# The up projection of a gated feed-forward block by Strassen's seven products of quarters

## The chip, the cores and the metric

The kernel runs on one core of one Trainium2 chip. Its engines are TensorE (PE; weight loads are shown as PEld), VectorE (DVE), ScalarE (ACT), GpSimd (POOL) and SyncE (SP, which here only issues DMAs). The metric is the device time of one execution in microseconds (us), lower is better. A matmul takes a stationary operand of 128x128 (the weights), a moving operand of 128 rows by some columns, and adds into PSUM.

## The reference, cut to what matters

One decoder layer is run for 512 prompt tokens and 64 sample tokens (8 sequences of 8), 576 columns in all. The model width is 1024 and D_FF is 2816. After retention, attention and the output projection comes the block that the change is about:

```
h = _rmsnorm(x, norm2_w)
ua, ub = jnp.split(h @ w_up, [D_FF], axis=-1)
buf = jnp.concatenate([conv_s0.astype(ua.dtype), ua], axis=1)
conv = conv_b
for j in range(CONV_W):
    conv = conv + buf[:, j:j + T] * conv_w[j]
x = x + (jax.nn.silu(conv) * ub) @ w_down
```

The outputs also hold the last two rows of `buf` (the convolution state) and a final norm of x.

## The kernel before, in words

All activations are kept transposed: 128 features on the partitions, 576 tokens along the free axis. A product in float32 is made of three passes of fp32r matmuls: both operands are split into a high part, rounded to fp32r, and the rest; high by high, high by low and low by high are added in PSUM.

Weights come as chunks of 128 columns by up to eight k tiles of 128 rows (`wraw`, 512 KB, three buffers). ACT rounds a chunk to `whi` (`w_split_hi`, L219) and DVE subtracts it from the raw one to make `wlo` (`w_split_lo`, L229), one chunk ahead of its use. `dense` (matmuls at L254) runs over the k tiles of a chunk: three passes by two halves of 288 tokens, six matmuls for each k.

The feed-forward block is done in two halves of 11 row tiles of D_FF each. For each tile f, called a slab here, `up` makes two dense products of eight k tiles, ua and ub: 2 x 48 = 96 matmuls. `up_post` then works on them beside the next slab: DVE scales ua by the norm's factor into `ue` (L1122, L1123), ACT and DVE do the three taps of the convolution (`cv`: L1126, L1130, L1131), ACT the silu (L1133); DVE scales ub into `g` (L1138), POOL multiplies it by the silu (L1141, L1142; DVE in the last slab of a half), ACT rounds the product (L1144) and DVE takes the rest (L1146). POOL also copies the convolution state in and out of `ue` (L1121, L1127, L1128). After 11 slabs, eight dense products with `w_down` (11 k tiles each) are added to x. The last of them, `last_down` (L1213), is cut into two groups of tokens so that the final norm overlaps it. `conv_state_in` (L1055) and `conv_state_out` (L1160) transpose the convolution state on PE.

The order of the work is fixed when the program is built: every engine has one queue and runs it in order, and semaphores hold an instruction back until what it reads is there and what it overwrites is no longer needed. The class `Merge` makes this order. It walks over generators that emit instructions and yield estimates of the time that PE and the other engines need, and lets the stream go on that is ready by these estimates. The run decides only the waits, not the order.

Of the kernel before, what the change touches and what calls it, by code (L numbers as in the profile page):

```python
# [18 lines left out]
P = 128  # L19
D = 1024  # L20
# [126 lines left out]
def decoder_step(ctx, tc, a):  # L147
# [29 lines left out]
    # ---- weights, streamed in order of use  # L177
# [3 lines left out]
    chunks = []  # L181
    IN_ORDER = [4 * sec + hp for hp in range(4) for sec in (1, 2, 0)]
    IN_ORDER += [4 * sec + hp for hp in range(4) for sec in (5, 4, 6)]
    IN_ORDER += [12 + hp for hp in range(4)]
    for m in IN_ORDER:
        chunks.append((("in", m, 0), a["w_in"], m, 0, 8))
    for m in range(8):
        chunks.append((("out", m, 0), a["w_out"], m, 0, 8))
    NFH = 11
    for half in range(2):  # L190
        for f in range(half * NFH, (half + 1) * NFH):
            chunks.append((("up", f, 0), a["w_up"], f, 0, 8))
            chunks.append((("up", NF + f, 0), a["w_up"], NF + f, 0, 8))
        for m in range(8):
            k0 = half * NFH
            chunks.append((("down", m, k0), a["w_down"], m, k0, k0 + 6))
            chunks.append((("down", m, k0 + 6), a["w_down"], m, k0 + 6, k0 + 11))
    raw, split = {}, {}
    state = {"load": 0, "use": 0}

    def w_load(upto):
        while state["load"] < min(upto, len(chunks)):
            w_load_part(state["load"], 0, 8)
            state["load"] += 1

    def w_load_part(i, c0, c1):
        _, w, m, k0, k1 = chunks[i]
        if i not in raw:
            raw[i] = wp.tile([P, 8, P], F32, name="wraw", tag="wraw", bufs=3)
        c1 = min(c1, k1 - k0)  # L210
        sp.dma_start(raw[i][:, c0:c1], wsrc(w, m, k0 + c0, k0 + c1))

    def w_split_hi(i, c0=0, c1=None):
        if i >= len(chunks) or i in split and c0 == 0:
            return
        if i not in split:
            split[i] = [wp.tile([P, 8, P], F32R, name="whi", tag="whi", bufs=2), None]
        c = slice(c0, c1 or chunks[i][4] - chunks[i][3])
        act.activation(split[i][0][:, c], raw[i][:, c], AF.Copy)  # L219

    def w_split_lo(i, c0=0, c1=None):
        if i >= len(chunks) or split[i][1] is not None and c0 == 0:
            return
        if split[i][1] is None:
            split[i][1] = wp.tile([P, 8, P], F32R, name="wlo", tag="wlo", bufs=2)
        hi, lo = split[i]
        n = chunks[i][4] - chunks[i][3]
        c = slice(c0, c1 or n)
        dve.tensor_sub(lo[:, c], raw[i][:, c], f32(hi[:, c]))  # L229
        if c.stop == n:  # L230
            raw.pop(i)

    def w_split(n):
        for i in range(state["use"], n):
            w_split_hi(i)
            w_split_lo(i)

    def w_next(key):
        i = state["use"]
        assert chunks[i][0] == key, (chunks[i][0], key)  # L240
        w_split(i + 1)
        state["use"] += 1
        return i, split.pop(i)

    def dense(ps, key, xhi, xlo, k0, k1, first, last, rows=None, made=None):
        """ps[:, C0 + n] (+)= sum over k of w[k, cols]^T x[k, n], in three exact-split passes."""
        i, (hi, lo) = w_next(key)
        w_split_hi(i + 1)
        for k in range(k0, k1):
            while made is not None and k not in made:  # L250
                yield None
            for wt, x in ((hi, xhi), (hi, xlo), (lo, xhi)):
                for s in range(2):
                    pe.matmul(ps[:, C0 + s * H2:C0 + (s + 1) * H2], wt[:, rows[k] if rows else k - k0], x[k][:, s * H2:(s + 1) * H2],  # L254
                              start=first and k == k0 and wt is hi and x is xhi,
                              stop=last and k == k1 - 1 and wt is lo)
            if k == k0 + 1:
                w_split_lo(i + 1)
            if k == k0 + 3:
                w_load(i + 4)  # L260
            yield 738.0, 0.0
# [4 lines left out]
    # ---- constants  # L266
# [31 lines left out]
    def rsqrt_steps(dst, v, t):  # L298
        """dst = v ** -0.5 for positive v: a seed from the exponent, then Newton's steps; t: scratch."""
# [24 lines left out]
    # ================= first norm  # L324
# [104 lines left out]
    def w_first():  # L429
        for i, h in ((0, 0), (1, 0), (0, 1), (1, 1)):  # L430
            w_split_hi(i, 4 * h, 4 * h + 4)
            yield 0.0, 700.0
            w_split_lo(i, 4 * h, 4 * h + 4)
            wk.add((i, h))
            yield 0.0, 900.0
# [3 lines left out]
    def in_first():  # L439
        """the first two tiles of columns advance together as x arrives"""  # L440
# [4 lines left out]
        for _, _, i, k in steps:  # L445
            while k not in split_k or (i, k // 4) not in wk:
                yield None
            hi, lo = split[i]
            for wt, x in ((hi, xhis), (hi, xlos), (lo, xhis)):
                for s in range(2):  # L450
                    pe.matmul(ps[i][:, C0 + s * H2:C0 + (s + 1) * H2], wt[:, k], x[k][:, s * H2:(s + 1) * H2],  # L451
                              start=k == 0 and wt is hi and x is xhis, stop=k == KD - 1 and wt is lo)
            if k == KD - 1:
                state["use"] += 1
                split.pop(i)
                if i == 0:
                    w_split_hi(2)
                    w_split_lo(2)
# [7 lines left out]
        yield from dense(first[m], ("in", m, 0), xhis, xlos, 0, KD, True, True)  # L466
# [8 lines left out]
    # ================= input projection, retention and dilated attention, by pairs of heads  # L475
# [13 lines left out]
    def natural(src, dst):  # L489
        """dst [token, tile, 128] = the transpose of src [128 features, T]"""  # L490
# [82 lines left out]
    def in_proj():  # L573
        for m in IN_ORDER:
# [3 lines left out]
            else:  # L578
# [3 lines left out]
                for c in dense(ps, ("in", m, 0), xhis, xlos, 0, KD, True, True):  # L582
# [9 lines left out]
    # ---- retention  # L592
# [12 lines left out]
    def retention():  # L605
        for hp in range(4):
# [13 lines left out]
            # scores, transposed: [key, query]  # L620
# [19 lines left out]
            # states after each chunk  # L640
# [13 lines left out]
            # outputs  # L654
# [21 lines left out]
            # group norm; the decay of a row only scales its statistics  # L676
# [29 lines left out]
            # states of the sample group  # L706
# [11 lines left out]
            # gate  # L718
# [13 lines left out]
    # ---- dilated attention, prompt  # L732
# [85 lines left out]
    def k_split(hp):  # L818
        """[k hi; k lo] of each head"""
# [26 lines left out]
    # ---- dilated attention, sample: four sequences at a time, each in 32 columns of the tensor engine  # L846
# [476 lines left out]
```

## Time and profile before

| what | us |
|---|---|
| three runs | 836.5, 838.94, 840.68; median 838.94 |
| span of the profiled execution | 838.0 |
| output projection | from about 345 to 396 |
| up, first half | from 396 to about 541 |
| down, first half | about 541 to 612 |
| up, second half | about 612 to 753 |
| down, second half | about 753 to 826 |
| final norm and last store | to 838.0 |

The page gives the profiled execution no time other than its span, which lies 0.9 us below the median of the runs. The slices of the page show PE busy at nine tenths or more nearly everywhere, and its granted clock at full except for one slice. Busy PE time counts the latency of overlapped matmuls too, so the pace is read from the count of matmuls in a stretch and not from the duration of one. An idle engine costs nothing unless another one waits for it.

### The profile page before, as it was taken

The numbers are of one execution on the slowest core, as the hardware profiler recorded it, in microseconds if no ns is written. First come the engines' busy times: TensorE is split into PE (matmuls) and PEld (weight loads), VectorE is DVE, ScalarE is ACT, GpSimd is POOL, SyncE is SP. The second block draws the span as 40 slices with busy tenths as digits, with TensorE's granted clock in tenths as the row PEclk, the third lists the DMA queues.
The fourth block names the chain that finished last, engine by engine and source line by source line (L and its number), as shares of the span: only waits on it lengthen the run. The fifth ranks groups of instructions, "written<-read, shape, count | busy, mean of one in ns | idle before, by whom it ended". The sixth has DMA issues, their size and how long they took to land.

```text
span 838.0 us, 16048 instructions
## 1 busy us (share of the span) xinstructions
PE 817.6 (98%) x6594; PEld 775.0 (92%) x6594; DVE 414.1 (49%) x796; ACT 295.2 (35%) x511; POOL 148.4 (18%) x234
## 2 busy tenths in 40 slices
PE   7999999998999999999999999999999999999995
PEld 6999999886887888999999999999999999999995
DVE  5664655655556456544555455432235545545333
ACT  5322321544536367234223333311223323332222
POOL 1312111020111113022212222100012222210111
PEclk9999999999999999899999999999999999999999
DMA  9355562667796873555256544453334445553213
GB/s 268 104 167 163 162 201 70 184 187 217 201 251 184 237 201 85 109 176 169 84 179 198 176 158 138 135 170 87 94 101 156 146 152 176 170 169 81 70 51 114
DMA packets 179534, 128.68 MB, mean 154 GB/s; under 512 B 15425, under 2 KB 176101, under 8 KB 178914
## 3 DMA queue, kind: packets, MB, share of 16 engines
q1 hardware_dynamic: 178308, 93.75, 40.1%
q10 hardware_dynamic: 928, 33.63, 11.0%
q8 instruction: 52, 0.85, 0.4%
q0 software_dynamic: 224, 0.28, 0.1%
q14 instruction: 22, 0.18, 0.1%
HBM read 121.52 MB, written 39.66 MB: 192 GB/s over the span
## 4 chain that ended last, share of the span: by engine, by line
PE 92%; DMA 3%; DVE 1%; ACT 1%; SPq 1%; issue 1%; POOL 0%; ACTq 0%; DVEq 0%; POOLq 0%
PE d L254 72%; PE m L877 2%; PE d L451 2%; PE m L923 2%; DMA kc<-in_cache_win_k_dram 1%; PE m L791 1%; PE d L887 1%; PE m L495 1%; PE m L804 1%; PE px L410 1%; PE m L1213 1%; PE px L254 1%; DMA csn<-in_state_conv_dram 1%; PE m L663 1%; PE m L764 1%
## 5 line engine op out<-in xcount | busy, mean ns | idle before, releaser
L219 ACT ACTIVATE whi<-wraw 128x1024 fp32r<-128x1024 f32 (+2 forms) x114 | 110.8, 972 | 372.2 <-issue 182.1
L229 DVE TENSOR_TENSOR wlo<-wraw,whi 128x1024 fp32r<-128x1024 f32 (+2 forms) x114 | 126.8, 1112 | 119.8 <-ACT whi L219 116.8
L254 PE MATMUL d<-bhi,whi 128*128 128x288 f32 x768 | 174.6, 309 | 0.0
L254 PE MATMUL d<-bhi,wlo 128*128 128x288 f32 x768 | 165.0, 297 | 0.0
L254 PE MATMUL d<-blo,whi 128*128 128x288 f32 x768 | 164.8, 296 | 0.0
L254 PE MATMUL d<-hhi,whi 128*128 128x288 f32 x704 | 150.9, 296 | 0.0
L254 PE MATMUL d<-hlo,whi 128*128 128x288 f32 x704 | 150.8, 296 | 0.0
L254 PE MATMUL d<-hhi,wlo 128*128 128x288 f32 x704 | 150.7, 296 | 0.0
L254 PEld LDWEIGHTS d<-bhi,whi 128*128 128x128 f32 x768 | 122.4, 191 | 5.3 <-issue 3.6
L254 PEld LDWEIGHTS d<-bhi,wlo 128*128 128x128 f32 x768 | 124.1, 189 | 0.0
L254 PEld LDWEIGHTS d<-blo,whi 128*128 128x128 f32 x768 | 124.1, 190 | 0.0
L254 PEld LDWEIGHTS d<-hhi,whi 128*128 128x128 f32 x704 | 113.4, 189 | 0.1
L254 PEld LDWEIGHTS d<-hhi,wlo 128*128 128x128 f32 x704 | 113.4, 189 | 0.0
L254 PEld LDWEIGHTS d<-hlo,whi 128*128 128x128 f32 x704 | 113.4, 189 | 0.0
L1122 DVE TENSOR_TENSOR ue<-d,rstd_b 128x512 f32<-128x512 f32 x22 | 15.2, 691 | 74.5 <-PE d L254 74.5
L1141 POOL TENSOR_TENSOR g<-g,cv 128x512 f32<-128x512 f32 x20 | 25.8, 1290 | 142.5 <-DVE g L1138 137.1
L785 POOL TENSOR_SCALAR s<-s,sc 128x128 f32<-128x128 f32 (+3 forms) x32 | 18.2, 578 | 141.7 <-DVE sc L783 140.4
L1038 POOL TENSOR_TENSOR acc<-acc,sq 128x576 f32<-128x576 f32 x13 | 21.4, 1646 | 111.5 <-ACT sq L1037 111.5
L1127 POOL COPY cout<-ue 128x2 f32<-128x2 f32 x22 | 5.7, 259 | 137.6 <-DVE ue L1122 137.6
L877 PE MATMUL m<-ident,kc 128*128 128x128 f32 x192 | 27.5, 277 | 2.1 <-DMA kc<-in_cache_win_k_dram 2.1
L878 DVE COPY kt<-m 128x384 f32<-128x384 f32 x32 | 17.8, 556 | 23.2 <-PE m L877 22.6
L878 ACT COPY kt<-m 128x384 f32<-128x384 f32 x32 | 15.3, 477 | 38.5 <-PE m L877 38.0
(261 smaller groups left out, 1033.7 us busy)
## 6 DMA issues: line engine op xcount, KB each, us to landing
wraw<-in_w_up_dram SPq DMA_DIRECT2D x44, 512.0 KB
wraw<-in_w_in_dram SPq DMA_DIRECT2D x26, 512.0 KB
kc<-in_cache_win_k_dram SPq DMA_DIRECT2D x32, 256.0 KB
vc<-in_cache_win_v_dram SPq DMA_DIRECT2D x32, 256.0 KB
wraw<-in_w_down_dram SPq DMA_DIRECT2D x16, 384.0 KB
wraw<-in_w_down_dram SPq DMA_DIRECT2D x16, 320.0 KB
kc<-in_cache_win_k_dram SPq DMA_DIRECT2D x64, 64.0 KB
vc<-in_cache_win_v_dram SPq DMA_DIRECT2D x64, 64.0 KB
```

What stands on the lines that cost most here:

```text
L219: act.activation(split[i][0][:, c], raw[i][:, c], AF.Copy)
L229: dve.tensor_sub(lo[:, c], raw[i][:, c], f32(hi[:, c]))
L254: pe.matmul(ps[:, C0 + s * H2:C0 + (s + 1) * H2], wt[:, rows[k] if rows else k - k0], x[k][:, s * H2:(s + 1) * H2], start=first and k == k ...
L410: pe.transpose(ps[:, s], xn[:r, j, k * P:(k + 1) * P], ident[:r, :r])
L451: pe.matmul(ps[i][:, C0 + s * H2:C0 + (s + 1) * H2], wt[:, k], x[k][:, s * H2:(s + 1) * H2], start=k == 0 and wt is hi and x is xhis, stop ...
L785: pool.tensor_scalar(s[:, :n], s[:, :n], c[:, 2:3], 1.0, op0=OP.mult, op1=OP.mult)
L877: pe.transpose(ps[:, j * P:(j + 1) * P], K[u, x][:, 3 * w + j], ident)
L878: (act.copy if w else dve.tensor_copy)(kt[:, w * 384:w * 384 + 384], ps[:, :384])
L923: pe.matmul(ps[x * 32:(x + 1) * 32, :P], pt[:n, j, x * 32:(x + 1) * 32], v, start=j == 0, stop=j == 6, tile_position=(0, x * 32))
L1038: pool.tensor_tensor(acc, acc, sq, op=OP.add)
L1122: dve.tensor_mul(u[:, 2:NP + 2], ya[:, :NP], rstd_b[:, :NP])
L1141: eng.tensor_tensor(g[:, :NP], g[:, :NP], c[:, :NP], op=OP.mult)
```

## The change: what it does

The up projection of a slab is taken as a 2x2 product of matrices. The weights are cut into A11 and A12 (k tiles 0 to 3 and 4 to 7 for ua) and A21 and A22 (the same for ub); h is cut into B11 and B12 (k tiles 0 to 3, token halves) and B21 and B22 (k tiles 4 to 7). Seven products of quarters (Winograd's form of Strassen's scheme), each of four k tiles by three passes by 288 tokens, take the place of eight. This needs four sums of weight quarters for each slab (S1 to S4, on POOL, `w_sum`) and four sums of quarters of h (T1 to T4, made once in `out_post`, on POOL, for the last pair of tiles on DVE). Results are put together from PSUM by three copies on ACT (`ct`) and three additions on DVE (into `y` and `z`; `z` is shown as `g`), partly while PE goes on adding to the same tile of PSUM.

Weights are split in quarters of four k tiles (128x512) throughout, two ahead and three in the feed-forward block, with five tiles for `whi` and `wlo` and a fourth raw buffer there. The down projection is done after 6, 14 and 22 slabs in chunks of 6, 8 and 8 k tiles, not twice 11. The output projection takes its tiles in the order 0, 4, 1, 5, 2, 6, 3, 7. The two copies of the convolution state into `cout` move from POOL to ACT, and its transposes become 4 on the way in and 5 on the way out in place of 22 and 22. `nfw`, the final norm's weight, is loaded before the last down stage and no longer before the output projection.

```diff
+    OUT_ORDER = [0, 4, 1, 5, 2, 6, 3, 7]
+    CHUNKS = [(0, 6), (6, 14), (14, 22)]
...
+    def add_slab(f):
...
+        quarters.extend([(i, slice(0, 4)), (i, slice(4, 8)), ("S2", f), ("S1", f), ("S3", f), ("S4", f),
+                         (i + 1, slice(4, 8))])
+        reads[i], reads[i + 1] = 5, 3
+        for n, which in enumerate(("S1", "S2", "S3", "S4")):
+            sums.setdefault(j - 5 + n, []).append((which, f, i))
...
+    def w_sum(which, f, i):
+
+        A11, A12, A21, A22 = raw[i][:, 0:4], raw[i][:, 4:8], raw[i + 1][:, 0:4], raw[i + 1][:, 4:8]
+        if which == "S3":
+            S[which, f] = A21
+            pool.tensor_tensor(A21, A11, A21, op=OP.subtract)
+            w_read(i)
             return
...
+        s = S[which, f] = state["ffn"][0].tile([P, 4, P], F32, name="ws", tag="ws", bufs=4)
+        if which == "S1":
+            pool.tensor_tensor(s, A21, A22, op=OP.add)
+            w_read(i + 1)
+        elif which == "S2":
+            pool.tensor_tensor(s, S["S1", f], A11, op=OP.subtract)
+            w_read(i)
+        else:
+            pool.tensor_tensor(s, A12, S["S2", f], op=OP.subtract)
+            w_read(i)
...
+    def w_begin(j):
+        for which in sums.pop(j, []):
+            w_sum(*which)
+        while state["hi"] <= min(j + ahead_of(), len(quarters) - 1):
+            if state["lo"] < state["hi"]:
+                w_lo(state["lo"])
+                state["lo"] += 1
+            w_hi(state["hi"])
+            state["hi"] += 1
...
+    def up(f, n, ghi, glo, made):
+
+        j = keys["up", f]
+        d, e = dtile(), mtile()
+        pa, pb, pc = d[:, :H2], d[:, 512:512 + H2], e[:, :H2]
+        y, z = tmp("y"), tmp("g")
+        ts = [fp.tile([P, H2], F32, name="ct", tag="ct", bufs=4) for _ in range(3)]
+        stage = []
+        for q, (dst, c) in enumerate(zip((pa, pb, pa, pc, pa, pc, pa), BQ)):
+            w_begin(j + q)
...
+                for wt, b in ((hi, xh), (hi, xl), (lo, xh)):
+                    pe.matmul(dst, wt[:, k], b[:, k], start=q in (0, 1, 3) and k == 0 and wt is hi and b is xh,
+                              stop=k == 3 and wt is lo, skip_group_check=True)
+                if k == 0:
+                    w_mid(j + q)
+                yield 385.0, 0.0
+            if q == 0:
+                act.copy(ts[0], pa)
+            elif q == 1:
+                dve.tensor_tensor(y[:, :H2], pb, ts[0], op=OP.add)
+            elif q == 2:
+                act.copy(ts[1], pa)
+            elif q == 3:
+                act.copy(ts[2], pc)
+            elif q == 4:
+                dve.tensor_tensor(z[:, H2:T], pa, ts[2], op=OP.add)
+            elif q == 5:
+                dve.tensor_tensor(y[:, H2:T], pc, ts[1], op=OP.add)
+                mg.add(up_post(f, n, pa, y, z, stage, ghi, glo, made), None, 4000.0 if f == 0 else 0.0)
+        stage.append(1)
...
-        dve.tensor_mul(u[:, 2:NP + 2], ya[:, :NP], rstd_b[:, :NP])
-        dve.tensor_mul(seqs(u, 2, TS), by_seq(ya[:, NP:]), by_seq(rstd_b[:, NP:]))
-        yield 0.0, 1800.0
-        c = fp.tile([P, UE], F32, name="cv", tag="cv", bufs=2)
+        dve.tensor_mul(u[:, 2:NP + 2], y[:, :NP], rstd_b[:, :NP])
+        dve.tensor_mul(seqs(u, 2, TS), by_seq(y[:, NP:T]), by_seq(rstd_b[:, NP:]))
+        yield 0.0, 1100.0
+        c = tmp("cv")
         act.activation(c[:, :L], u[:, 0:L], AF.Identity, scale=convw[:, 0, f:f + 1], bias=convb[:, f:f + 1])
-        pool.tensor_copy(cout[:, f, 0:2], u[:, NP:NP + 2])
-        pool.tensor_copy(by_seq(cout[:, f, 2:]), seqs(u, TS, 2))
-        yield 0.0, 1800.0
+        act.copy(cout[:, 0:2, f], u[:, NP:NP + 2])
+        act.copy(by_seq(cout[:, 2:, f]), seqs(u, TS, 2))
+        while not stage:
+            yield None
+        dve.tensor_mul(z[:, :H2], pa, rstd_b[:, :H2])
+        dve.tensor_mul(z[:, H2:T], z[:, H2:T], rstd_b[:, H2:])
+        yield 0.0, 900.0
```

VectorE's queue over one slab of the first up stage before (`wlo` is the low part of a weight chunk, `ue` the scaled ua, `cv` the convolution, `g` the scaled ub, `blo` the low part of the product):

```order
L1122 TENSOR_TENSOR ue1_4418<-d_5340,rstd_b_73 128x512
L1123 TENSOR_TENSOR ue1_4418<-d_5340,rstd_b_73 128x8x8
L229 TENSOR_TENSOR wlo_5418<-wraw_5307,whi_5401 128x1024
L1146 TENSOR_TENSOR blo_4932<-g_5364,bhi_4930 128x576
L1130 SCALAR_TENSOR_TENSOR cv_5435<-ue1_4418,vec_71,cv_5435 128x592
L1131 SCALAR_TENSOR_TENSOR cv_5435<-ue1_4418,vec_71,cv_5435 128x592
L229 TENSOR_TENSOR wlo_5483<-wraw_5372,whi_5468 128x1024
L1138 TENSOR_TENSOR g_5491<-d_5400,rstd_b_73 128x576
```

And now, from one slab's last convolution step to the next one's scaling of `y` (`ws` is a sum of weight quarters, `d` and `m` are PSUM, `y` and `ct` are in SBUF):

```order
L1271 SCALAR_TENSOR_TENSOR cv_5790<-ue1_4543,vec_71,cv_5790 128x592
L290 TENSOR_TENSOR wlo_5827<-wraw_5565,whi_5822 128x512
L1241 TENSOR_TENSOR y_5796<-d_5794,ct_5798 128x288
L290 TENSOR_TENSOR wlo_5847<-ws_5750,whi_5842 128x512
L290 TENSOR_TENSOR wlo_5868<-wraw_5565,whi_5863 128x512
L290 TENSOR_TENSOR wlob_5888<-wraw_5606,whib_5883 128x512
L1281 TENSOR_TENSOR blo_5141<-g_5644,bhi_5140 128x576
L1247 TENSOR_TENSOR g_5797<-d_5794,ct_5800 128x288
L290 TENSOR_TENSOR wlo_5909<-wraw_5606,whi_5904 128x512
L1249 TENSOR_TENSOR y_5796<-m_5795,ct_5799 128x288
L290 TENSOR_TENSOR wlo_5928<-ws_5861,whi_5923 128x512
L1258 TENSOR_TENSOR ue0_4541<-y_5796,rstd_b_73 128x512
```

Eight instructions of a slab have become seventeen: behind these rows follow the rest of `ue`, one more `wlo`, the two scalings of `g` and the two convolution steps (L1270, L1271). The scaling of `ue` reads SBUF twice now, where before one operand was in PSUM. On ACT the order there is `cv` (L1262), two copies into `cout`, the next `whi`, the first `ct`, another `whi`, the silu (L1273), another `whi`, the second `ct` (L1243).

GpSimd's queue over one slab before (`cout` is the convolution state out):

```order
L1141 TENSOR_TENSOR g_5491<-g_5491,cv_5435 128x512
L1142 TENSOR_TENSOR g_5491<-g_5491,cv_5435 128x64
L1121 COPY ue0_4416<-csT_4413 128x8x2
L1127 COPY cout_4414<-ue0_4416 128x2
L1128 COPY cout_4414<-ue0_4416 128x16
```

And now, in the slab whose rows of VectorE stand above:

```order
L269 TENSOR_TENSOR ws_5840<-wraw_5717 128x512
L1276 TENSOR_TENSOR g_5644<-g_5644,cv_5790 128x512
L1277 TENSOR_TENSOR g_5644<-g_5644,cv_5790 128x64
L272 TENSOR_TENSOR ws_5861<-ws_5840,wraw_5606 128x512
L264 TENSOR_TENSOR wraw_5717<-wraw_5606,wraw_5717 128x512
L275 TENSOR_TENSOR ws_5902<-wraw_5606,ws_5861 128x512
L1257 COPY ue0_4541<-csT_4525 128x8x2
```

The product for slab f now stands between the first sum of a slab and the other three, and the copy into `ue`, which `cv` on ACT waits for, stands behind the last sum.

## Rows read from the trace of the kernel before

**Rows 1.** The page's parts 1 and 4: busy time of each engine; the chain by engine.
```profile
PE 817.6 (98%) x6594; PEld 775.0 (92%) x6594; DVE 414.1 (49%) x796; ACT 295.2 (35%) x511; POOL 148.4 (18%) x234
...
PE 92%; DMA 3%; DVE 1%; ACT 1%; SPq 1%; issue 1%; POOL 0%; ACTq 0%; DVEq 0%; POOLq 0%
```

**Rows 2.** Windows: busy us of each engine from 402 to 541, the first up stage.
```profile
402.00:541.00 139.00, 139.00 (x1043) 138.73 (x1043) 69.54 (x103) 43.91 (x54) 32.52 (x53) 1.00 0.48 151
```

**Rows 3.** Chain of waits in order of time: start, us, what.
```profile
408.12 349.43 PE d L254 x2622
...
819.39 1.76 PE m L1213 x12
```

**Rows 4.** Timeline of ACT in the first up stage: start, us, operation, [idle before <-releaser].
```profile
442.52 1.06 ACT L219 ACTIVATE whi<-wraw 128x1024 fp32r<-128x1024 f32 x1 [4.75 <-issue]
443.49 0.66 ACT L1144 CAST bhi<-g 128x576 fp32r<-128x576 f32 x1
...
444.05 0.88 ACT L1126 ACTIVATE cv<-ue,vec 128x592 f32<-128x592 f32 x1
...
455.32 1.06 ACT L219 ACTIVATE whi<-wraw 128x1024 fp32r<-128x1024 f32 x1 [4.75 <-issue]
```

**Rows 5.** Timeline of DVE in the same slab.
```profile
443.62 1.23 DVE L229 TENSOR_TENSOR wlo<-wraw,whi 128x1024 fp32r<-128x1024 f32 x1
444.76 0.75 DVE L1146 TENSOR_TENSOR blo<-g,bhi 128x576 fp32r<-128x576 f32 x1
445.43 0.82 DVE L1130 SCALAR_TENSOR_TENSOR cv<-ue,vec,cv 128x592 f32<-128x592 f32 x1
446.29 0.84 DVE L1131 SCALAR_TENSOR_TENSOR cv<-ue,vec,cv 128x592 f32<-128x592 f32 x1
```

**Rows 6.** Groups by line and form: count | busy us, mean ns | idle before.
```profile
L229 DVE TENSOR_TENSOR wlo<-wraw,whi 128x512 fp32r<-128x512 f32 x4 | 2.8, 690 | 2.1 <-ACT whi L219 2.1
...
L1228 DVE TENSOR_TENSOR xT<-m,xT 128x256 f32<-128x256 f32 x1 | 0.4, 425 | 0.8 <-PE m L1213 0.8
...
L219 ACT ACTIVATE whi<-wraw 128x512 fp32r<-128x512 f32 x4 | 2.5, 635 | 5.3 <-DMA wraw<-in_w_in_dram 5.3
...
L1133 ACT ACTIVATE cv<-cv 128x592 f32<-128x592 f32 x22 | 15.1, 685 | 2.9 <-DVE cv L1131 2.9
...
L795 ACT COPY pt<-m 128x256 f32<-128x256 f32 x4 | 1.4, 362 | 1.1 <-PE m L791 1.1
...
L1246 ACT ACTIVATE stat<-stat 128x3 f32<-128x3 f32 x1 | 0.2, 207 | 0.2 <-DVE stat L1243 0.2
...
L1141 POOL TENSOR_TENSOR g<-g,cv 128x512 f32<-128x512 f32 x20 | 25.8, 1290 | 142.5 <-DVE g L1138 137.1 <-ACT cv L1133 5.4
```

**Rows 7.** Timeline of POOL, three places.
```profile
330.89 1.90 POOL L532 TENSOR_TENSOR roT<-roT,t 128x576 f32<-128x576 f32 x1 [3.11 <-ACT t L528]
...
443.62 1.28 POOL L1128 COPY cout<-ue 128x16 f32<-128x16 f32 x1
...
808.95 1.42 POOL L1038 TENSOR_TENSOR acc<-acc,sq 128x576 f32<-128x576 f32 x1 [7.88 <-ACT sq L1037]
```

**Rows 8.** Timeline of DVE beside the first and the third of them.
```profile
331.88 1.52 DVE L1011 TENSOR_TENSOR blo<-aoT,bhi 128x576 fp32r<-128x576 f32 x1 [0.38 <-ACT bhi L1009]
...
333.81 0.76 DVE L1011 TENSOR_TENSOR blo<-aoT,bhi 128x576 fp32r<-128x576 f32 x1
...
810.09 0.69 DVE L1173 TENSOR_TENSOR yn<-m,nfw 128x512 f32<-128x512 f32 x1 [1.34 <-PE m L1170]
```

**Rows 9.** Timeline of PE: transposes of the convolution state, in and out.
```profile
348.84 2.21 PE L1055 MATMUL m<-ident,csn 16*128 16x16 f32 x22 [1.50 <-DMA csn<-in_state_conv_dram]
...
757.38 0.60 PE L1160 MATMUL m<-ident,cout 128*18 128x128 f32 x4
```

**Rows 10.** Windows, as in Rows 2, at two interruptions of PE.
```profile
194.00:196.00 2.00, 0.98 (x9) 0.71 (x7) 0.93 (x2) 0.89 (x3) 0.00 (x0) 1.00 0.90 235
...
352.00:356.00 4.00, 4.00 (x19) 4.00 (x18) 0.41 (x1) 0.00 (x0) 0.00 (x0) 0.50 0.21 52
```

More of the change, by code (lines that the diff above doesn't have):

```diff
@@ new lines, in decoder_step, with w_tile @@
+    for m in IN_ORDER:
+        add_dense(("in", m), a["w_in"], m, 0, 8)
+    for m in OUT_ORDER:
+        add_dense(("out", m), a["w_out"], m, 0, 8, True)
+    for f0, f1 in CHUNKS:
+        for f in range(f0, f1):
+            add_slab(f)
+        for m in range(8):
+            add_dense(("down", m, f0), a["w_down"], m, f0, f1)
+    raw, split, S = {}, {}, {}
+    state = {"load": 0, "hi": 0, "lo": 0, "auto": False, "ffn": None}
+    def w_tile(which, j):
+        if state["ffn"] and (j - state["ffn"][1]) % 5 == 4:
+            return state["ffn"][0].tile([P, 4, P], F32R, name=which + "b", tag=which + "b", bufs=1)
+        return wp.tile([P, 4, P], F32R, name=which, tag=which, bufs=4)
@@ L201, in w_load @@
     def w_load(upto):
-        while state["load"] < min(upto, len(chunks)):
+        while state["load"] < min(upto, len(raws)):
             w_load_part(state["load"], 0, 8)
@@ L233, in w_split, with w_read @@
[L233 to L261, printed above, removed]
+    def w_read(i):
+        reads[i] -= 1
+        if not reads[i]:
+            raw.pop(i)
+        if state["auto"]:
+            while state["load"] < len(raws) and len(raw) < (4 if state["ffn"] else 3):
+                w_load(state["load"] + 1)
@@ new lines, in w_hi, with w_lo @@
+    def w_hi(j):
+        if j < len(quarters) and j not in split:
+            src = w_src(j)
+            n = src.shape[1]
+            split[j] = [w_tile("whi", j), None]
+            act.activation(split[j][0][:, :n], src, AF.Copy)
+    def w_lo(j):
+        if j < len(quarters) and split[j][1] is None:
+            src = w_src(j)
+            n = src.shape[1]
+            split[j][1] = w_tile("wlo", j)
+            dve.tensor_sub(split[j][1][:, :n], src, f32(split[j][0][:, :n]))
+            x, c = quarters[j]
+            if isinstance(x, str):
+                S.pop((x, c))
+                if x == "S3":
+                    w_read(quarters[keys["up", c]][0] + 1)
+            else:
+                w_read(x)
@@ new lines, in ahead_of, with w_mid @@
+    def ahead_of():
+        return 3 if state["ffn"] else 2
+    def w_begin(j):
[7 more added lines that the diff above has]
+            state["hi"] += 1
+    def w_mid(j):
+        while state["lo"] < state["hi"]:
+            w_lo(state["lo"])
+            state["lo"] += 1
@@ new lines, in dense @@
+    def dense(ps, key, xhi, xlo, k0, k1, first, last, made=None):
+        j, k = keys[key], k0
+        while k < k1:
+            w_begin(j)
+            if split[j][1] is None:
+                w_mid(j)
+            hi, lo = split.pop(j)
+            c = quarters[j][1]
+            for x in range(c.stop - c.start):
+                while made is not None and k not in made:
+                    yield None
+                for wt, b in ((hi, xhi), (hi, xlo), (lo, xhi)):
+                    for s in range(2):
+                        pe.matmul(ps[:, C0 + s * H2:C0 + (s + 1) * H2], wt[:, x],
+                                  b[k][:, s * H2:(s + 1) * H2],
+                                  start=first and k == k0 and wt is hi and b is xhi,
+                                  stop=last and k == k1 - 1 and wt is lo)
+                if x == 0:
+                    w_mid(j)
+                k += 1
+                yield 738.0, 0.0
+            j += 1
@@ L1138, in up_post @@
[L1138 to L1147 removed]
+        yield 0.0, 700.0
```

298 lines of the change are left out of this document (155 added, 143 removed).

## The prediction, written before the run

> **What bounds the kernel now.** I read the page's busy times and chain first: PE is busy for 98% of the span and is 92% of the chain that ended last [rows 1]. The windows show how: from 402 to 541 us PE runs without a gap at full clock while DVE is busy for 69.5 of 139 us and POOL for 32.5 [rows 2]. The chain in order of time gives the pace: 2622 matmuls in 349.43 us, 133.3 ns each [rows 3]. One slab takes 12.80 us, from one `whi` on ACT at 442.52 to the next of its kind at 455.32 [rows 4], and that is 96 x 133.3 ns. So each matmul taken out of the up stage is worth 133.3 ns as long as nothing else becomes the bound.
>
> **What the change removes.** A slab has 7 x 12 = 84 matmuls instead of 96: 11.2 us instead of 12.8. Adding into one PSUM tile twelve times in a row costs nothing extra: `last_down` does so with 320 columns and takes 1.76/12 = 147 ns [rows 3], 13.3 ns more than 288 columns, which is what 32 columns take at 2.4 GHz. Over 22 slabs 35.2 us are on offer.
>
> **What it adds on DVE.** DVE starts one instruction about 0.09 us before the last one's listed end (443.62 to 444.76 with 1.23 listed), but a step that reads the one before starts behind it (445.43 to 446.29) [rows 5]. The seven `wlo` of 512 columns have a listed 0.69 [rows 6], so 0.60 each: 4.2. Three additions and two scalings of 288 columns: the row of 256 has 0.425 [rows 6]; with 32 columns more at about 1.05 ns (1.23 for 1024 against 0.69 for 512) 0.46, less 0.09 is 0.37: 1.85 for five. `blo` 0.67, from its start to the next one's [rows 5]. `ue` 0.60 and about 0.2: 0.8. Two convolution steps at 0.86: 1.72. Together 9.24 us in a slab.
>
> **A wait that is new.** In the new order DVE's `wlo` behind `ue` needs a `whi` that stands on ACT behind `cv` and two copies into `cout`, and `cv` needs `ue`. DVE stands for `cv` 0.88 less 0.09 [rows 4], two small copies of about 0.12 (0.207 listed for three elements), `whi` 0.635 [rows 6] and two handovers of about 0.05: 1.8 us. Behind it are queued `g`, the convolution steps, and with them the silu. The second `ct` waits behind the silu on ACT, and PE's fifth quarter, which adds to the same PSUM, waits for that `ct`.
>
> **What it adds on POOL, and who waits for it.** Four sums join the product, all of 128x512 with two inputs, as the product that takes 1.29 [rows 6]: with small ones 6.7 us in a slab. That looks hidden on an engine with a load of a quarter, but the trace says otherwise. At 331.88 a `blo` on DVE took 1.52 instead of the 0.76 of its like at 333.81 [rows 8]: POOL's product of 330.89 ran until 332.79 [rows 7], and `blo` ended 0.61 behind that, its own time less 0.15. The other way round POOL's copy of 16 elements at 443.62 took 1.28 [rows 7], until 0.05 behind the end of the `wlo` that started with it [rows 5]. So where both read SBUF, they take turns by whole instructions, and a handover saves about 0.15. An instruction of DVE with one operand in PSUM is not held: at 810.09 it took 0.69 [rows 8] inside POOL's addition of 808.95 to 810.37 [rows 7].
> The Trainium skill, "SBUF — State Buffer", Who interferes with whom, has this as a rule: a VectorE instruction with two SBUF inputs and a GpSimd instruction that reads SBUF exclude each other, the later one blocking fully. By that rule every `wlo` can be held, and the slab is the one worked out below; if the two places above were exceptions, it would be the second rival's.
>
> **The slab.** I put t = 0 where the second convolution step of slab f ends. The silu runs to 0.8, the product holds SBUF to 2.2, and DVE's third instruction, a `wlo`, first waits 0.4 for its `whi` behind the silu and then 0.7 for the product. From here S2, S3 and S4 alternate with `wlo`, `wlo` and `blo`; they hold DVE up by 1.1, 1.1 and, as an addition from PSUM runs beside S4, 0.7; the small ones 0.1. S1 of the next slab holds up another 0.9 if its weights have landed, else it falls into the 1.8 us in which DVE waits for ACT. So DVE's queue needs 9.24 + 1.8 + 0.4 + 2.6 + 1.0 = 15.0 to 15.9 us for one slab; I take 15.5. The bounds: below, nothing but the taking of turns: DVE's two-operand instructions 7.3 and POOL's 5 x 1.14 and 0.3 are 13.3 us. Above, all five of POOL's held against DVE in full: 9.24 + 1.8 + 0.4 + 5.7 = 17.1. PE has 11.2 us of work in it and waits for the rest.
>
> **The three chunks.** From a chunk's first matmul to the end of its first slab's convolution: six quarters at 1.6, an addition and a `wlo`, `ue`, the 1.8 on ACT, `wlo`, two scalings and two steps: 16.5 us. Then come n - 2 slabs at 15.5, and a last one without sums (weights of the down stage need none): 9.24 + 1.8 + 0.4 + 0.7 = 12.1. Then silu 0.69, product on DVE 0.8, rounding 0.66 and handovers: 2.4. That is 93.0 for n = 6 and 124.0 for n = 8, 341.0 in all. The first down product can run ahead of the last slab by n - 1 k tiles of 0.8 us, 19 in all: 15.2. The up stage so takes 325.8 us instead of 22 x 12.8 = 281.6: +44.2. (With twice 11 tiles, 8 us of matmuls cover that tail; with 6 only 4.)
>
> **The rest.** From the output projection into the first slab, T2, T1 and T4 of the last pair are made on DVE: 15 instructions, about 6.7 us, beside three additions of squares at 1.42 [rows 7] and four sums on POOL. If six of these seven hold DVE up, T4 is there 13.6 us after the last product, and PE wants it at 9.6: +4, and +1 for the norm's chain behind it in the same queue; bounds 0 and +8. The convolution state cost PE a wait of 1.5 and 2.21 us for 22 transposes [rows 9], and behind them the clock stood at half: 352 to 356 us at 0.50 [rows 10]; some 22 matmuls at 240 instead of 133 ns, 2.4 us. Four transposes and a load that no longer stands behind `nfw`: up to -5.7, at least -1.8; I take -4.5. On the way out 17 transposes fewer at 0.60/4 us [rows 9]: -2.5. PE stands about 4 us at the first change to the down stage (8 us of tail against 4), and I count one fall of the clock, +2.5. Extra additions into x (a third round) lie on DVE under the down products, 5 to 6 us each. The split of weights into quarters adds instructions before the block where DVE is under 60% busy: 0.
> Sum: 838.0 + 44.2 + 5 + 2.5 - 4.5 - 2.5 = 882.7. The profiled span lies 0.9 below the median of the runs: 884.
>
> **Rivals.** First, PE stays the bound, since DVE and POOL have room by their busy shares [rows 2]: -35.2, tails 6.2 long against 4.0, 5.6 and 5.6 (+3.4), +2 at the start, -7 for the convolution state: 801. Against it: rows 7 and 8, and 9.2 us of DVE with 1.8 of waiting leave nothing free in 11.2.
> Second, SBUF does not hold the engines up, and the loop through the queues decides: two quarters 3.4, addition 0.4, `wlo` 0.6, `ue` 0.8, ACT 1.8, `wlo` 0.6, scalings 0.74, steps 1.72, silu 0.7, `whi` 0.55, `ct` 0.4 are 11.7, with a little queueing 11.9. That is 22 x 0.9 = 20 less, tails +9, start +2, -7.5: 821, faster than before. It decides if fewer than two of the five POOL instructions hold up DVE. Against it: both directions of the hold stand in the rows.
> Third, PE's gaps of 1 to 2.5 us in each slab bring the clock down. Then a slab's matmuls take 84 x 240 ns = 20.2 us; in half of the 16 steady slabs +38, in all +75: 922 to 959. Against it: in 194 to 196 PE was busy for half of the time, and the clock stayed at 1.00 [rows 10]. The Trainium skill, "TensorE: Matmul & The Clock Gate", Part 1: The HAM clock gate, says that the low clock is the default and activity lifts it; no run here shows where a PE busy for 70% with short gaps falls.
>
> **How the numbers follow.** My forecast has 0.77, the first rival 0.05, the second 0.08, the third 0.06; 0.04 is left for sums in between, 825 to 842. The forecast's own range is 842 to 908: 13.3 us in the 16 steady slabs takes off 35, no loss at the start and the whole gain at the convolution state 6 more; 16.5 us, +8 at the start and two more falls of the clock add 24. That is also the range for 8 in 10. No change means within 0.5%, 4.2 us, about what can be told here: 0.03. Faster: both first rivals and a bit of the rest, 0.14; slower 0.83.
>
> **What would show it.** In the profile after, slabs of 15 to 16 us with PE busy for some 11 of them; PE's waits before the third, fifth and seventh quarter, on ACT's `ct` and DVE's `g`; `wlo` of 512 columns with a mean near 1 us instead of 0.69, and the sums on POOL well over 1.29. I am wrong if `wlo` stays at 0.69 beside running sums, or if a slab takes under 12.8; right in the hold but wrong in size if it takes 13 to 14.

## The result, and the profile after

The changed kernel takes 932.16 us (median of 4 runs, 928.76 to 934.31), the kernel before 838.62 beside it: a ratio of 1.111, 95% interval 1.108 to 1.115. It is slower, as forecast, but by 94 us where 45 were forecast, and the time lies above the top of the range, 908.

The page of the profile after, its busy times, the granted clock and the chain of waits, to be read against [rows 1]:

```profile
PE 813.5 (88%) x6295; PEld 755.7 (82%) x6295; DVE 570.6 (62%) x1095; ACT 377.9 (41%) x809; POOL 262.0 (28%) x288
...
PEclk9999999999999999989999999798899999989998
...
PE 62%; DVE 20%; ACT 7%; issue 7%; SPq 1%; DMA 1%; ACTq 1%; POOL 0%; POOLq 0%; DVEq 0%
```

PE has fallen from 92% of the chain to 62%, DVE has risen from 1% to 20%. No engine is full: DVE, the busiest of the others, works for 62% of the span. That alone proves nothing, as an average over stages, but it suits a loop through several queues better than one engine at its limit; the chain of one slab below shows the loop.

The ends of the convolutions give the pace of the slabs. These are the second steps (start, length) of the first and the last slab of chunk 1, of chunk 2 and of chunk 3:

```profile
430.46 0.83 DVE L1271 SCALAR_TENSOR_TENSOR cv<-ue,vec,cv 128x592 f32<-128x592 f32 x1
...
506.45 0.83 DVE L1271 SCALAR_TENSOR_TENSOR cv<-ue,vec,cv 128x592 f32<-128x592 f32 x1
...
564.19 0.83 DVE L1271 SCALAR_TENSOR_TENSOR cv<-ue,vec,cv 128x592 f32<-128x592 f32 x1
...
678.73 0.83 DVE L1271 SCALAR_TENSOR_TENSOR cv<-ue,vec,cv 128x592 f32<-128x592 f32 x1
...
746.20 0.83 DVE L1271 SCALAR_TENSOR_TENSOR cv<-ue,vec,cv 128x592 f32<-128x592 f32 x1
...
860.18 0.83 DVE L1271 SCALAR_TENSOR_TENSOR cv<-ue,vec,cv 128x592 f32<-128x592 f32 x1
```

From these ends the miss can be put in its places. The span, of the fastest of the four runs, is 927.0 us against a sum of 882.7.

| place | forecast, us | measured, us | miss, us |
|---|---|---|---|
| first convolution of all ends at | 413.0 | 431.3 | +18.3 |
| 16 steady intervals | 16 x 15.5 | 16 x 16.19 | +11.0 |
| the last interval of each chunk | 3 x 12.1 | 15.4, 14.3, 15.8 | +9.2 |
| first matmul to first convolution, chunks 2 and 3 | 2 x 16.5 | 2 x 18.8 | +4.6 |
| the rest | | | +1.2 |

The first end is forecast from 396 in the kernel before, 4.5 us less for the convolution state, 5 more on the way in and 16.5 for the slab.

Now one slab. The chain of waits in order of time (start, us, what), from the end of one convolution to the end of the next:

```profile
565.63 0.38 DVE y L1241
...
566.05 1.86 PE d L1233 x12
567.91 1.60 PE m L1233 x12
...
569.64 0.52 ACTq L597
570.16 0.32 ACT whi L283
...
570.50 0.84 DVE wlo L290
571.34 1.42 DVE blo L1281
...
573.03 0.44 DVE g L1247
...
575.04 0.60 DVE ue L1258
...
576.96 0.52 ACT whib L283
...
578.93 0.76 DVE cv L1270
...
579.74 1.62 issue
```

It goes around: DVE's addition `y`, then two quarters on PE (3.46 us), then ACT, whose `whi` stands behind the two copies `ct` of those quarters (in this slab behind one DMA issue of 0.52, too), then DVE's `wlo`, and everything behind it in DVE's queue up to `ue`, ACT's tap and its `whi`, the convolution, and the next `y`. The holds are in it too. DVE in the same slab (start, length, what it stood for):

```profile
566.31 1.35 DVE L290 TENSOR_TENSOR wlob<-ws,whib 128x512 fp32r<-128x512 f32 x1 [0.31 <-ACT whib L283]
568.91 0.72 DVE L290 TENSOR_TENSOR wlo<-wraw,whi 128x512 fp32r<-128x512 f32 x1 [1.24 <-ACT whi L283]
570.50 0.84 DVE L290 TENSOR_TENSOR wlo<-wrawb,whi 128x512 fp32r<-128x512 f32 x1 [0.87 <-ACT whi L283]
571.26 1.84 DVE L1281 TENSOR_TENSOR blo<-g,bhi 128x576 fp32r<-128x576 f32 x1
...
577.50 0.69 DVE L290 TENSOR_TENSOR wlob<-ws,whib 128x512 fp32r<-128x512 f32 x1 [1.73 <-ACT whib L283]
...
579.71 1.73 DVE L1271 SCALAR_TENSOR_TENSOR cv<-ue,vec,cv 128x592 f32<-128x592 f32 x1
```

and POOL beside it:

```profile
570.75 1.74 POOL L275 TENSOR_TENSOR ws<-wrawb,ws 128x512 f32<-128x512 f32 x1
...
579.55 1.26 POOL L269 TENSOR_TENSOR ws<-wraw 128x512 f32<-128x512 f32 x1 [6.38 <-DMA wraw<-in_w_up_dram]
```

`blo`, started inside S4, takes 1.84 us instead of the 0.76 of [rows 8], and the convolution step 1.73 behind the start of S1 instead of 0.83. So the hold is real, in both directions, as [rows 7, 8] had it. The slab adds up: 9.24 of DVE's own, holds of 1.08, 0.90, 0.67 and, on two `wlo` together, 0.20, and waits of 0.31, 1.24, 0.87 and 1.73, together 16.24; the interval is 16.42.

What PE waited for in the stretch of chunk 2 (us in all, times, longest):

```profile
PE d L1233 <- DVE y L1241: 13.4, 8, 2.8
PE d L1233 <- ACT ct L1239: 9.9, 8, 1.9
```

The first is the wait before the third quarter, the second the one before the second quarter. Over the whole kernel they are 39.9 and 27.0 us. Neither pair shares an address: the second quarter writes `d` from column 512 on while `ct` reads columns 0 to 287, and the third writes 0 to 287 while `y` reads from 512 on.

### The profile page after: what moved, and what is told of

Its sections match the earlier page's. It is cut to its first block, busy times and chain, and to the rows that moved or that the text cites. A ratio compares the mean times of both kernels' runs of the same rounds, so it can differ in the third digit from the quotient of the medians.

```text
span 927.0 us, 16218 instructions
## 1 busy us (share of the span) xinstructions
PE 813.5 (88%) x6295; PEld 755.7 (82%) x6295; DVE 570.6 (62%) x1095; ACT 377.9 (41%) x809; POOL 262.0 (28%) x288
## 4 chain that ended last, share of the span: by engine, by line
PE 62%; DVE 20%; ACT 7%; issue 7%; SPq 1%; DMA 1%; ACTq 1%; POOL 0%; POOLq 0%; DVEq 0%
PE d L331 33%; PE d L1233 7%; DVE wlo L290 5%; PE m L1233 5%; ACT whi L283 2%; DVE ue L1258 2%; DVE blo L1281 2%; PE m L957 2%; DVE cv L1270 2%; PE d L529 2%; PE m L1003 1%; PE m L884 1%; PE m L575 1%; DVE g L1267 1%; PE d L967 1%
## 5 line engine op out<-in xcount | busy, mean ns | idle before, releaser
L1233 PE MATMUL d<-T,whi 128*128 128x288 f32 x712 | 154.5, 310 | 60.1 <-DVE y L1241 31.9
L290 DVE TENSOR_TENSOR wlo<-wraw,whi 128x512 fp32r<-128x512 f32 (+1 forms) x152 | 122.3, 807 | 100.5 <-ACT whi L283 100.4
L1233 PEld LDWEIGHTS d<-T,whi 128*128 128x128 f32 x712 | 117.6, 195 | 70.6 <-DVE y L1241 36.4
L283 ACT ACTIVATE whi<-wraw 128x512 fp32r<-128x512 f32 (+1 forms) x152 | 93.8, 623 | 58.0 <-PE d L331 37.8
L1233 PE MATMUL d<-T,wlo 128*128 128x288 f32 x356 | 108.3, 304 | 0.0
L290 DVE TENSOR_TENSOR wlo<-ws,whi 128x512 fp32r<-128x512 f32 x51 | 49.5, 971 | 34.1 <-ACT whi L283 34.1
L1233 PEld LDWEIGHTS d<-T,wlo 128*128 128x128 f32 x356 | 70.2, 197 | 0.0
L1233 PE MATMUL m<-T,whi 128*128 128x288 f32 x264 | 58.0, 313 | 0.0
L1262 ACT ACTIVATE cv<-ue,vec 128x592 f32<-128x592 f32 x22 | 19.4, 881 | 74.1 <-DVE ue L1259 74.1
L1233 PEld LDWEIGHTS m<-T,whi 128*128 128x128 f32 x264 | 47.0, 208 | 0.0
L1233 PE MATMUL m<-T,wlo 128*128 128x288 f32 x132 | 40.8, 309 | 0.0
```

The lines of the kernel that those rows point to most:

```text
L283: act.activation(split[j][0][:, :n], src, AF.Copy)
L290: dve.tensor_sub(split[j][1][:, :n], src, f32(split[j][0][:, :n]))
L1233: pe.matmul(dst, wt[:, k], b[:, k], start=q in (0, 1, 3) and k == 0 and wt is hi and b is xh, stop=k == 3 and wt is lo, skip_group_check=True)
L1262: act.activation(c[:, :L], u[:, 0:L], AF.Identity, scale=convw[:, 0, f:f + 1], bias=convb[:, f:f + 1])
```

## Experiments

The kernel before ran beside all of them. The table has the median, the ratio to the kernel before with its 95% interval, the mean of the 12 steady intervals of chunks 2 and 3, the mean of the three last intervals, and the end of the first convolution. The quoted expectations call the theory that DVE's queue and POOL's holds alone set the slab H, and the theory of the loop L.

| kernel | us | ratio | slab | last | first |
|---|---|---|---|---|---|
| the change | 932.2 | 1.111 (1.108 to 1.115) | 16.54 | 15.2 | 431.3 |
| sums left out | 894.8 | 1.064 (1.060 to 1.069) | 14.55 | 15.7 | 424.2 |
| three sums twice | 979.6 | 1.165 (1.160 to 1.171) | 19.02 | 15.2 | 438.1 |
| own PSUM tile | 907.2 | 1.079 (1.073 to 1.084) | 15.77 | 12.4 | 429.9 |
| `wlo` later | 901.6 | 1.073 (1.067 to 1.079) | 15.49 | 12.9 | 426.8 |
| own tile and `wlo` later | 861.9 | 1.027 (1.024 to 1.030) | 13.79 | 10.6 | 426.7 |
| both, sums left out | 812.8 | 0.970 (0.965 to 0.974) | 11.13 | 11.0 | 418.6 |
| filler on PE | 929.0 | 1.108 (1.104 to 1.111) | 16.32 | 14.7 | 431.2 |
| both, sums on DVE | 842.0 | 1.006 (1.004 to 1.008) | 12.71 | 10.5 | 422.0 |
| both, sums and product on DVE | 835.9 | 0.997 (0.995 to 0.999) | 12.44 | 10.1 | 419.0 |
| kernel before, convolution state of the change | 833.2 | 0.993 (0.991 to 0.996) | | | |

**The sums left out.**

```diff
-        quarters.extend([(i, slice(0, 4)), (i, slice(4, 8)), ("S2", f), ("S1", f), ("S3", f), ("S4", f), ...])
+        quarters.extend([A11, A12, A11, A12, A21, A21, A22])
...
```

> Leaves out the four sums S1 to S4 of each slab: the seven products take plain quarters in their place (so the output is another one), everything else stands, and two more buffers hold the raw weights that then live longer. Theory H (POOL's sums hold DVE up, and DVE's queue sets the slab): the 16.4 us of a steady slab lose the holds seen in the profile after (about 0.7 to 1.1 us on each of two or three DVE instructions), so about 14.2 us a slab, and about 932 - 22 x 2.1 = 885 us; `wlo` of 512 columns has its mean back near 0.70. Rival L (the slab is a loop from DVE over PE's quarters and ACT's queue back to DVE, and most holds fall into waits that are there anyway): no more than 1 us a slab, 905 to 930 us.

894.8 us, 37 less. Where H wanted 47 and L at most 27, it lies halfway; the slab lost 2.0 us, near the 2.2 of H. The group of `blo` shows the hold gone (count, busy, mean ns of one, idle before); the profile after, then this run:

```profile
L1281 DVE TENSOR_TENSOR blo<-g,bhi 128x576 fp32r<-128x576 f32 x22 | 24.2, 1102 | 2.2 <-ACT bhi L1279 2.2
...
L1279 DVE TENSOR_TENSOR blo<-g,bhi 128x576 fp32r<-128x576 f32 x22 | 16.6, 753 | 2.2 <-ACT bhi L1277 2.2
```

The `wlo` made from `wraw`, at a mean of 799, mix in the projections ahead of the block; the 86 made from `wrawb`, a buffer of the block alone, have 749. But without sums DVE's own 9.24, the forecast waits of 2.2 and a hold by the product of 0.7 are 12.1 us, and the slab stays at 14.55: something other than the holds is in it.

**Three sums twice.**

```diff
+            for _ in range(2):
                 pool.tensor_tensor(s, A21, A22, op=OP.add)
...
```

> POOL computes S1, S2 and S4 of each slab twice, the second time over the first; nothing else changes. POOL has 7 of 16.4 us to do in a slab, so it has the room. Theory H: three more instructions of 1.3 us that read SBUF, each holding up DVE by 0.5 to 1.1, give 1.5 to 3 us a slab more: 960 to 995 us. Rival L: the added holds fall into DVE's waits: under 10 us more, 932 to 942.

979.6 us: 47 more for 66 POOL instructions, 0.72 each. POOL has the room in time, and still each of them costs, as H says. That the sums come later is not the reason: no instruction of ACT waits for one in this profile. `blo` now:

```profile
L1284 DVE TENSOR_TENSOR blo<-g,bhi 128x576 fp32r<-128x576 f32 x22 | 33.0, 1502 | 2.2 <-ACT bhi L1282 2.2
```

**An own PSUM tile for the second product.**

```diff
-        d, e = dtile(), mtile()
-        pa, pb, pc = d[:, :H2], d[:, 512:512 + H2], e[:, :H2]
+        pa, pb, pc = dtile()[:, :H2], mtile()[:, :H2], mtile()[:, :H2]
```

> The second product gets a PSUM tile of its own; now it is the second bank of the tile whose first bank holds the first product, and the profile after shows PE waiting before the second quarter for `ct`, which reads the first bank, and before the third for `y`, which reads the second: 27.0 and 39.9 us in all. Neither pair shares an address. Theory L: these waits come from the tile being tracked as a whole, and they tie PE into the loop; without them they shrink to under 20 us together, DVE's waits for `whi` behind `ct` shrink with them, a slab takes about 14 us, the stretches of half clock that follow them go, and the time is 885 to 905. Theory H (DVE's queue alone decides): PE waits elsewhere instead, 925 to 935.

907.2 us, 2 above L's range. What PE waited for over the whole kernel:

```profile
PE d L1232 <- DVE g L1246: 34.0, 16, 2.2
PE d L1232 <- ACT ct L1242: 19.2, 18, 1.8
...
PE d L1232 <- ACT ct L1238: 4.2, 6, 1.2
```

The wait for `y` is gone and that for the first `ct` is 4.2 instead of 27.0, so both came from two PSUM banks being one tile. Part of the time stands now before the fifth and the seventh quarter, in waits on data that PE does need: the slab gained 0.8 us and not 2.4. The Trainium skill, "PSUM — Partial Sum Buffer", PSUM bank collisions raise a hardware error, lets two engines work in different banks side by side; the run agrees: in one slab the second quarter runs from 568.11 us on while `ct` reads the bank of the first from 568.31 to 568.71.

**`wlo` one quarter later.**

```diff
     def w_mid(j):
-        while state["lo"] < state["hi"]:
+        while state["lo"] < (max(j + 1, state["hi"] - 1) if state["ffn"] else state["hi"]):
```

> In the feed-forward block the `wlo` of a quarter is issued one quarter later than now, so that DVE no longer reaches it while its `whi` still stands in ACT's queue. The profile after shows DVE idle for 4 to 5.7 us in a slab before `wlo`, waiting for `whi`. Theory L: these waits go, what is left of the loop (four quarters on PE 6.9, two additions and `wlo` 1.6, `ue` 0.74, ACT 1.0, convolution 2.4 with one hold of 0.9, `wlo` and `y` 1.0) is 14 us, and the time about 890 to 905. Theory H in its pure form (DVE has 9.2 us of its own and 2.8 of holds): 12 to 12.5 us a slab, 850 to 870. If the waits only move to other instructions, 925 to 935.

901.6 us, in L's range; the slab of 15.5 is 1.5 above the 14 of L, and PE's two false waits are still there, 33.4 us for `ct` and 15.3 for `y`, 48.7 together instead of 66.9.

**Both edits.**

> Both edits at once: the second product in a PSUM tile of its own, and `wlo` issued one quarter later. Alone they gave 907.2 and 901.6 us against 932.2 of the change as it is. Theory L (a loop through all three queues, of which each edit opens one side): the gains add up or more, since only DVE's queue with POOL's holds is left: 9.2 us of its own, 2.8 of holds and about 1 of waits make 13 us a slab, and the time 860 to 880. Rival (the two edits take away the same wait): no better than the better one, 895 to 905.

861.9 us: 25.0 and 30.6 us less alone, 70.2 together. Together they give more than the sum of the two, as theory L has it: each opens one side of the loop. What is left is H in its pure form, two engines that take turns, and DVE has no time free: the window of 13 us (columns as in [rows 2]), then DVE's rows:

```profile
566.00:579.00 13.00, 9.80 (x71) 9.17 (x70) 12.96 (x17) 7.08 (x15) 7.82 (x7) 1.00 0.57 195
...
569.98 1.77 DVE L290 TENSOR_TENSOR wlo<-wraw,whi 128x512 fp32r<-128x512 f32 x1
...
572.39 1.77 DVE L290 TENSOR_TENSOR wlob<-wraw,whib 128x512 fp32r<-128x512 f32 x1
574.09 1.83 DVE L1280 TENSOR_TENSOR blo<-g,bhi 128x576 fp32r<-128x576 f32 x1
575.84 0.45 DVE L1246 TENSOR_TENSOR g<-d,ct 128x288 f32<-128x288 f32 x1
```

and POOL in the same time:

```profile
571.88 1.73 POOL L272 TENSOR_TENSOR ws<-ws,wrawb 128x512 f32<-128x512 f32 x1
573.57 1.73 POOL L264 TENSOR_TENSOR wraw<-wrawb,wraw 128x512 f32<-128x512 f32 x1
575.26 1.79 POOL L275 TENSOR_TENSOR ws<-wrawb,ws 128x512 f32<-128x512 f32 x1
```

Read the ends: a POOL sum ends, some 0.55 later a DVE instruction ends, then the next sum. An instruction of each takes 1.7 us, the sum of 1.26 and 0.6 less the 0.15 that a handover saves; `g`, which reads PSUM, runs in 0.45 inside S4.

**Both edits without the sums.**

> The same two edits, and the four sums left out as before (plain quarters in their place, another output). Nothing but the product on POOL then holds DVE up, so DVE has 9.9 us in a slab and PE 11.2. Theory: PE becomes the bound, 11.2 to 12 us a slab; first and last slabs of the chunks and the way in still cost some 25 us against the kernel before, so 825 to 845 us. If a slab stays above 13 us, something else than the two false waits and the holds is in the loop.

812.8 us, below the expected range, and PE is the bound at 11.13 us a slab, the 84 matmuls at 133 ns. So what stood last between the slab and PE came with the sums. This run can't tell the holds from the rest that went with the sums (their waits for loads; two raw buffers were added too); the two runs with the sums on DVE below can, since they keep the sums and the four buffers.

**Filler on PE.**

```diff
             xh, xl = TH[c]
+            for _ in range((0, 8, 14, 0, 0, 0, 0)[q]):
+                pe.matmul(e[:, H2:512], TH["B11"][0][:, 0, :P], TH["B11"][0][:, 0, :512 - H2], ...)
```

> The change as it is, but before the second quarter PE gets 8 and before the third 14 matmuls of 224 columns whose result nobody reads, into columns of PSUM that are free (about 0.1 us each, so 0.8 and 1.5 us where the profile after shows waits of 1.2 and 1.8 on average). In the profile after the clock falls to half after 11 of those waits, and about 150 matmuls of the up stage take 240 instead of 133 ns, 16 us. Theory K (these matmuls stand in the loop, and work in the wait keeps the clock up): 916 to 924 us, no stretch of half clock in the slabs. Rival (the half clock lies beside other waits, or the added matmuls cost as much as they save): 928 to 940.

929.0 us, and the intervals of the two ratios overlap: the difference is a few us at most. Yet the clock did what the theory asked. Chunk 2 in the profile after, then with the filler (busy us of each engine, granted clock behind them):

```profile
546.00:683.00 137.00, 109.88 (x720) 104.96 (x719) 93.22 (x142) 58.24 (x122) 52.07 (x47) 0.91 0.39 127
```

```profile
546.00:683.00 137.00, 121.62 (x895) 117.25 (x894) 97.99 (x142) 58.76 (x123) 54.80 (x45) 0.99 0.40 130
```

Theory K falls as far as time goes: at 0.99 instead of 0.91 the slab is 16.32 instead of 16.54. The filler does not hide a gain there: in 17 of the 22 slabs both quarters behind it start 0.05 us after the `ct` or `y` that they wait for. In the other five, the first of each chunk among them, it delays a quarter, by 0.9 us at most and some 4 us in all. What PE gains, it waits for in part before the seventh quarter; the profile after, then with the filler:

```profile
PE d L1233 <- DVE g L1247: 8.9, 8, 2.8
...
PE d L1236 <- DVE g L1250: 18.2, 16, 2.2
```

**The sums on DVE.**

```diff
-            pool.tensor_tensor(s, A21, A22, op=OP.add)
+            dve.tensor_tensor(s, A21, A22, op=OP.add)
...
```

> The two edits of the queue (own PSUM tile, `wlo` a quarter later), and the four sums issued on DVE in place of POOL, at the same places in the program. On POOL a sum takes about 1.75 us in that version and holds each DVE instruction beside it by 0.8 to 1.1; on DVE it costs about 0.60. Theory H (two operands in SBUF on both engines take turns): DVE's queue falls from 13.5 to 9.2 + 2.4 + 0.7 for the product + a little, 12.4 us a slab, and the time from 862 to 838 to 848. Rival (the sums were hidden on POOL after all, or S1, which waits for its weights to land, now stops DVE): DVE gets 2.4 us longer or stands for the load, 870 to 900.

842.0 us: giving 88 more instructions to the engine that is the bound saves 20 us.

**Sums and product on DVE.**

```diff
-            sums.setdefault(j - 5 + n, []).append((which, f, i))
+            sums.setdefault(j - 3 + n, []).append((which, f, i))
...
-        eng = dve if made["last"] == f else pool
+        eng = dve
...
```

> As the run with the sums on DVE, but each sum two places later in the program, so that its weights have landed, and the product of gate and convolution on DVE too: POOL has only copies of 16 columns left. Theory H: DVE has 9.2 + 2.4 + 0.8 = 12.4 us in a slab and nothing holds it; PE has 11.2. So 12.4 to 12.8 us a slab, 836 to 845 us, level with the kernel before, for the gain on PE is then given back on DVE. Rival (the later sums keep the raw weights longer, and loads come late): over 13 us a slab, 850 to 870.

835.9 us at 12.44 us a slab, both at the lower edge of what H has. Chunk 2 in its windows, columns as above: DVE is busy for 83.69 of 85 us, POOL for 3.85.

```profile
530.00:615.00 85.00, 81.87 (x582) 77.43 (x582) 83.69 (x158) 49.58 (x105) 3.85 (x8) 1.00 0.55 177
```

**The kernel before with the convolution state of the change** (4 and 5 transposes, the norm's weights loaded later):

> The kernel before with three side parts of the change alone: the convolution state goes in by 4 transposes instead of 22 and out by 5 instead of 22, and the last norm's weights are loaded behind the last up slab instead of ahead of the convolution state. By the terms of the prediction -4.5 (bounds -1.8 and -5.7) and -2.5 us: 830 to 834. Rival (PE's wait there belongs to the norm and not to these loads, and the 17 transposes less on the way out lie beside the down products): within 2 us of the kernel before.

833.2 us, 6.9 less than the kernel before beside it: the sum of the terms, -7.0, holds. By the profiled executions the way in gives more than its term and the way out less: the first convolution ends 5.3 us earlier (409.13 for 414.45), and the span is 7.1 shorter. PE's wait for `csn` is gone, and the transposes in take 0.5 instead of 2.2 us [rows 9]:

```profile
L1055 PE MATMUL m<-ident,csn 88*128 88x88 f32 x4 | 0.5, 238 | 0.0
```

It is the fastest of those that compute the reference, if by little: the last version of Strassen's scheme, which has this part too, is 0.4% behind it by the two ratios, and their intervals touch.

## Why the prediction was right in the sign and wrong in the size

**What bounds, and what is on offer: right.** With both edits and without the sums a slab takes 11.13 us, against 11.2 forecast.

**What it adds on DVE: right.** The 9.24 us, with 2.4 for four sums and 0.8 for the product, make 12.44, and the run with all of them on DVE measures 12.44.

**POOL's holds: right in kind, too large here.** Both directions stand in the profile after; doubling three sums cost 47 us, leaving four out gave 37. In the slab shown they come to 2.85 us and in the next to 1.8, where the sum had 3.6 to 4.5. The signs that it named are there: `wlo` made from a sum has a mean of 971 ns, S1 on POOL 1490. The Trainium skill, "SBUF — State Buffer", Who interferes with whom, has DVE with two SBUF inputs and GpSimd's reads exclude each other; the rows agree, and add the price, 0.7 to 1.1 us of DVE for one sum that DVE itself makes in 0.60.

**A wait that is new: two of four found.** The 1.8 behind the first tap of the convolution, on ACT, and the 0.4 behind the silu are there, 1.73 and 0.31. The prediction followed `whi` on ACT only behind `cv`. Two more `whi` stand behind `ct`, which wait for PE's third and fourth quarter: 1.24 and 0.87 in the slab shown, 2.52 and 1.15 in the next.

**The slab: this is the step that failed.** The sum added up one queue: own work, two waits taken as constants, and holds. Its three terms in the table make 24.8 of the 44.3 us missed. It gives 15.5 with sums, and 16.2 was measured, which looks close; but too much for holds and too little for waits nearly cancelled. The last slab of a chunk, which has no sums, shows the fault: by the same sum 12.1, measured 15.2 on average. In the last one of chunk 2 the hold is 0.67, but DVE's waits come to 4.20 as in the slab shown, and in that of chunk 1 to 5.7, where the sum has 2.2. The slab is a loop DVE, PE, ACT, DVE, and PE was in it because the second and the third quarter waited for reads of the other bank of their tile. The sum had PE wait before the third, fifth and seventh quarter, and only as a consequence. Two edits that touch neither a count of instructions nor a duration took off 70 us; with them the last slabs take 10.6.

**The rest: the way in, too small by far, and the largest of the misses.** The forecast had +5 and a bound of +8; the first convolution ended 18.3 us late. Of that, 4.6 stand ahead of the block: its first matmul starts at 396.06 where the sum has 391.5, and PE is late long before that: the last transposes of attention (L990 in the kernel after) start at 330.7, their like in the kernel before with the convolution state of the change at 325.2. PE waits there for DVE and POOL where it did not before, 1.18 us at 163 and 1.32 at 166. So the term of 0 for the split in quarters is wrong as well, or something else of the change costs time there; that was not tried.

The other 13.7 stand between the first matmul and the end of the first convolution, 35.2 us where the sum has 21.5. PE's waits from 392 to 432 us add up to 12.4, of which 1.7 lie in the second slab already (us in all, times, longest):

```profile
PE d L1233 <- DVE T L1165: 3.7, 1, 3.7
PE d L1233 <- DVE g L1247: 2.8, 1, 2.8
PE d L1233 <- DVE y L1241: 2.3, 2, 1.2
...
PE d L1233 <- ACT T L1163: 1.4, 1, 1.4
```

The first and the last are for instructions that prepare T. The second, for `g`, is the norm's chain, taken at +1: its small steps fill DVE's queue ahead of `g` from 417.5 to 420.0. Loop and holds are in it too: from the first matmul on, the stretch takes 35.2 us with the own tile alone, 30.9 with `wlo` later, 30.4 without the sums, and 24.2 with both edits and no sums. How that splits into the single waits was not tried.

**The rivals.** The first, PE as the bound, needed two false waits and the sums away, and then came to 812.8, not 801, with the slab as it has it; the 12 more lie outside the steady slabs. The second was nearest to the truth in kind, a loop through the queues with two quarters of PE in it. But it came to PE by the second `ct`, before the fifth quarter, where the chain shown comes to it by `y`, before the third, and it had one `whi` in place of the waits found and no holds: 11.9 us for 16.2. The third has the measured time in its range, 922 to 959, but by luck. It was half right: the clock falls after many of PE's waits in a slab. The rows of one: behind a wait of 0.83 us the granted clock is 1.00 (577.8 to 579.5 us), and a pair of matmuls takes 0.43 us; behind 2.81 us of waiting it is 0.54 (582.46 to 584.5), close to the lower level of 1.2 GHz, and a pair takes 0.69.

```profile
578.31 0.43 PE L1233 MATMUL d<-T,whi 128*128 128x288 f32 x2
...
582.46 0.73 PE L1233 MATMUL d<-T,whi 128*128 128x288 f32 x2 [2.81 <-DVE y L1241]
...
583.23 0.69 PE L1233 MATMUL d<-T,whi 128*128 128x288 f32 x2
```

The filler shows that this cost next to nothing: about 0.2 us in a slab, where the rival had 4.7 in a slab at half clock.

## What to carry to other kernels

Where a change makes engines read each other's results several times in one step, add up the loop and not the fullest queue: write down for each waiting instruction what is queued behind it, go on until you are back where you began, and check whether each wait is for an address or only for a tile that two banks share. A sum hidden on GpSimd is not hidden when it takes the SBUF reads that VectorE needs: here it cost 0.7 to 1.1 us against 0.6 on VectorE itself. And take the cheap side parts of a large change on their own: here they were all that made the kernel faster.

## What had not been expected of the hardware

Two engines that both read SBUF alternate one by one where both queues are full: in the stretch shown a pair of 128x512 instructions, one on each, takes about 1.7 us. And a clock at 0.91 over a whole chunk was worth about 0.2 us in a slab: PE, at 0.99, waited longer for the others.
